# Weight requests queued behind the reads of turned softmax weights, in a two-layer attention trunk on one core

## The chip, the cores and the metric

One core of a Trainium2 chip runs the whole program. The metric is device time in microseconds (us) of one execution. The kernel before took 809.79 us (median of 3 runs, 808.65 to 813.39).

## The reference, cut to what matters

Two layers of a gated hybrid trunk on 512 rows of 1024 values, all in float32. Each layer normalises its rows, multiplies them by one wide matrix, and feeds the pieces to two branches: a sparse attention with eight heads, and a gated linear attention with four heads. The branches are multiplied up, gated, added, multiplied by an output matrix, normalised and added to the input.

```python
def _layer(x, ...):
    h = _rms(x, g_pre)
    proj = h @ w_in
    ...
    o_nsa = _nsa_attention(q_rope, q_nope, k_cmp, v_cmp, k_slc, v_slc, k_win, v_win, nsa_gate)
    o_nsa = o_nsa * jax.nn.silu(p_nz)
    ...
    o_gla = (o_gla * jax.nn.silu(p_gr...))
    m_nsa, m_gla = jnp.split(jax.nn.sigmoid(p_mg), N_BRANCHES, axis=-1)
    y = m_nsa * (o_nsa @ w_up_nsa) + m_gla * (o_gla @ w_up_gla)
    return x + _rms(y @ w_out, g_post)
```

The sparse attention of a row is three softmax branches (compressed, selected, window), each weighted by a gate. The selected and the window branch are what this change touches: their softmax weights are computed with the rows on the partitions, and have to be turned so that the keys lie on the partitions before they can multiply the values.

## The kernel before, in words

**Weights.** All weights of a layer lie packed in one tensor `wpk`, in the order of their use, as 128x1024 blocks (512 KB) or 128x512 blocks (256 KB). `load(i)` (L125) requests block i: one DMA on SyncE's queue (SP) into one of three `raw` buffers (L136), then a cast on ScalarE that keeps the high part (`A.copy`, L153) and a subtraction on VectorE that leaves the low part (L154), into two of six `hl` buffers. `split3` (L175) then makes three matmuls of each 128x128 piece: high by high (L177), high by low (L178), low by high (L179). So the first matmul of a block needs its cast, and the third needs its subtraction. `get` (L171) is called when a product starts, and requests two blocks ahead of the one that it hands out.

**Attention.** For each of four head pairs p, a step of compressed attention (`cmp_steps`, L887) is followed by four steps of `attn_steps` (L980): two halves of the rows (ip = 0, 1) by two branches (br = 0, 1). A step multiplies queries by keys (`scores`, L957), makes softmax weights (`weigh`: L970 on VectorE, the exponential L972 on ScalarE, L974 and L975 on VectorE), and turns them (`turn`, L924). Turning is a 32x32 transposition on VectorE into a tile `T` (L935), a write of that tile to DRAM (`tp`, L940) and four reads that bring it back with the keys on the partitions (`PT`, L943). The four reads are 224 KB each for the second half of the rows and 96 KB each for the first. After them the weights multiply the values (L998). In what follows "the write" is L940 and "the reads" are the four of L943.

**Order.** TensorE's order is written by hand: `go` makes one step of attention, and `fill` puts pieces of weight products between the steps, from a queue of products. A product's tanh (L593 or L736) or its copy out (L698) on ScalarE follows its last matmul. On the other engines and on SP a scheduler orders the instructions by what it thinks will be ready, unless an `issue_after` puts one behind another on its engine. The list `back` holds the reads issued so far in a layer; in `turn` a write already stands behind the latest read (L939).

**Names.** In the layer's order of blocks the ones that this text speaks of are q3, nz2, nz3 (query and gate of heads), mgg0 to mgg7 (512 KB) alternating with ug0 to ug7 (256 KB), and mgn0, un0 and so on. In the first layer q3 is `raw_1684`, nz2 `raw_1780`, nz3 `raw_1866`, ug1 `raw_2214`, mgg2 `raw_2283`, ug3 `raw_2494`, ug4 `raw_2642`, mgg5 `raw_2690`, ug6 `raw_2901`, ug7 `raw_3049`, mgn0 `raw_3097`. A product of mgg multiplies the tile `hT`, one of ug the tile `oT`.

Of the kernel before, what the change touches and what calls it, by code (L numbers as in the profile page):

```python
# [67 lines left out]
def trunk(ctx, tc, x, wpk, sp, gvec, cs, wa, out):  # L68
# [23 lines left out]
    def new(pl, shape=(128, 512), dt=F32, tag=None, bufs=None):  # L92
        cnt[0] += 1
        kw = {} if bufs is None else {"bufs": bufs}
        return sb[pl].tile(list(shape), dt, tag=tag or pl, name=f"{tag or pl}_{cnt[0]}", **kw)
# [10 lines left out]
    dma = nc.sync.dma_start  # L106
# [13 lines left out]
    POS = {k: i for i, k in enumerate(SEQ)}  # L120
    ready = {}
    issued = [0]
    first_w, behind = [], []

    def load(i):  # L125
        l, n = SEQ[i]
        off, w = OFF[n]
        src = wpk[l][:, off:off + w]
        if n.startswith("w1"):
            t = [new("a"), new("a")]  # L130
            for h in range(2):
                dma(t[h], src[:, h * 512:(h + 1) * 512])
            ready[l, n] = t
            return
        r = new("raw", (128, 1024))
        dma(r[:, :w], src)  # L136
        if i < 3:
            ready[l, n] = (new("hl", (128, 1024), F32R), new("hl", (128, 1024), F32R))
            first_w.append((r, w) + ready[l, n])
            return  # L140
        if n.startswith("wo") or n in ("gv0", "gv3", "gq0", "gk0"):
            pl = "a" if n < "wo4" and n > "wo" else "oT"
            parts = []
            for h in range(2):
                H, Lo = new(pl, dt=F32R), new(pl, dt=F32R)
                rr = r[:, h * 512:(h + 1) * 512]
                A.copy(H, rr)
                V.tensor_sub(Lo, rr, H.bitcast(F32))
                parts.append((H, Lo))
            ready[l, n] = parts  # L150
            return
        H, Lo = new("hl", (128, 1024), F32R), new("hl", (128, 1024), F32R)
        A.copy(H[:, :w], r[:, :w])  # L153
        V.tensor_tensor(Lo[:, :w], r[:, :w], H[:, :w].bitcast(F32), op=OP.subtract)  # L154
        ready[l, n] = (H, Lo)
# [9 lines left out]
    def issue(i):  # L165
        while issued[0] <= min(i, len(SEQ) - 1):
            with behind_tokens() if issued[0] < 7 else nullcontext():
                load(issued[0])
            issued[0] += 1
# [142 lines left out]
    for l in range(L):  # L312
# [21 lines left out]
        def fill(us):  # L334
            credit[0] += us
            while credit[0] > 0.3 and queue:
                credit[0] -= step(*queue[0])

        def step(name, gen):
            try:  # L340
                return next(gen)
            except StopIteration:
                queue.pop(0)
                done.add(name)
                return 0.0

        def need(name):
            while name not in done:
                step(*queue[0])
# [381 lines left out]
        def up(f, gate, wn, src, then):  # L731
            th = []

            def sig(o):
                th.append(new("th"))
                A.activation(th[0], o, AF.Tanh, scale=0.5)  # L736

            yield from fm(l, f"{gate}{f}", hT, sig)
            w = get(l, f"{wn}{f}")
            u = ps("mm")  # L740
            for k in range(4):
                sl = slice(k * 128, (k + 1) * 128)
                split3(u, (w[0][:, sl], w[1][:, sl]), src[k], k == 0, k == 3)
                if k == 3:
                    then(th[0], u)
                yield 0.64
# [172 lines left out]
            mm(acc, vbd[1], pcT, start=False, stop=False, skip_group_check=True)  # L919
            yield  # L920

        PT, TT, held, back, nsc = {}, {}, {}, [], [0]

        def turn(p, br, i, pps):  # L924

# [96 lines left out]
        def take_un(f):  # L1022
            def g(th, u):
                t_ = new("p")
                V.scalar_tensor_tensor(t_, th, 1.0, u, op0=OP.add, op1=OP.mult)  # L1025
                G.tensor_tensor(t_, t_, y2[f], op=OP.add)  # L1026
                if f < 3:
                    both = new("PT", (128, 2, 512), F32R, tag="PT1") if f < 2 else new("T", (128, 2, 512), F32R, tag="T1")
                    H, Lo = both[:, 0], both[:, 1]
                else:  # L1030
                    H, Lo = new("g", dt=F32R), new("g", dt=F32R)
                A.mul(H, t_, 0.5)
                V.scalar_tensor_tensor(Lo, t_, 0.5, H.bitcast(F32), op0=OP.mult, op1=OP.subtract)
                yT.append((H, Lo))
            return g


        for n in range(len(steps)):
# [21 lines left out]
                go(n - 2)  # L1060
            fill(f4[3])
        need("ug7")

        uns = [up(f, "mgn", "un", oTn, take_un(f)) for f in range(8)]
        for f in range(2):
# [9 lines left out]
        src = x if l == 0 else x1  # L1075
# [112 lines left out]
```

## Time and profile before

| | |
|---|---|
| median of 3 runs | 809.79 us (808.65 to 813.39) |
| the profiled execution | 808.68 us, span of its instructions 807.0 us |
| TensorE busy | 789.5 us, 98% |
| VectorE busy | 553.5 us, 69% |
| ScalarE busy | 354.4 us, 44% |
| mean granted TensorE clock | 0.997 of 2.4 GHz |

The span is the time from the first to the last instruction; the execution is 1.7 us longer. A row of a group of instructions gives the line, the engine, the operation, the output and input tiles, shapes and count, then busy time and mean ns of one, then the idle time of the engine just before them and what ended it.

### The profile page before, as it was taken

The page shows a single profiled execution, that of the slowest core. Times are in us where ns is not written, and L with a number is a line of the kernel's source. Part 1 is how long each engine was busy: PE and PEld are TensorE (multiplying, and loading weights), DVE is VectorE, ACT ScalarE, POOL GpSimd, SP SyncE. Part 2 cuts the span into 40 slices and gives each one's busy share as a digit, 9 for nine tenths or more (in the row PEclk, how much of TensorE's full clock was granted, in tenths as well). Part 3 has the DMA queues.
Part 4 walks back from the last instruction along what each step waited for, and adds up shares of the span by engine and source line. Part 5 has one row for each costly group of instructions (what it writes and reads, how often), then busy time and mean ns, then how long its engine had stood idle before and what let it go on. Part 6 is the DMA issues. An engine that isn't in the chain of part 4 may idle for free. (4 is left out here: it accounts for less than half of the span.)

```text
span 807.0 us, 12043 instructions
## 1 busy us (share of the span) xinstructions
PE 789.5 (98%) x4262; PEld 644.4 (80%) x4262; DVE 553.5 (69%) x1274; ACT 354.4 (44%) x731; POOL 97.6 (12%) x117
## 2 busy tenths in 40 slices
PE   8999999999989999999999999999999999999996
PEld 5888788887878887888898878888877788788885
DVE  6753749999998945645574366589999987366223
ACT  5671236554554524442356413556555444245211
POOL 3000024000010102211010102311000101032100
PEclk9999999999999999999999999999999999999998
DMA  6641124367676773446246121234767677545222
GB/s 233 229 147 58 53 67 130 105 191 217 183 236 204 235 227 119 153 153 223 79 129 212 52 78 54 83 114 149 223 201 215 214 212 222 171 157 158 78 105 79
DMA packets 54272, 124.04 MB, mean 154 GB/s; under 512 B 6562, under 2 KB 23490, under 8 KB 54212
## 3 DMA queue, kind: packets, MB, share of 16 engines
q1 hardware_dynamic: 54064, 123.01, 48.4%
q8 instruction: 34, 0.56, 0.3%
q10 hardware_dynamic: 148, 0.27, 0.1%
q14 instruction: 26, 0.21, 0.1%
HBM read 94.94 MB, written 25.17 MB: 149 GB/s over the span
## 5 line engine op out<-in xcount | busy, mean ns | idle before, releaser
L177 PE MATMUL ps_mm<-hT,hl 128*128 128x512 f32 x544 | 217.5, 400 | 0.0
L178 PE MATMUL ps_mm<-hT,hl 128*128 128x512 f32 x544 | 212.5, 391 | 0.0
L179 PE MATMUL ps_mm<-hT,hl 128*128 128x512 f32 x544 | 212.3, 390 | 0.0
L153 ACT CAST hl<-raw 128x1024 fp32r<-128x1024 f32 (+3 forms) x107 | 97.6, 915 | 138.3 <-PE ps_mm L178 99.9
L154 DVE TENSOR_TENSOR hl<-raw,hl 128x1024 fp32r<-128x1024 f32 (+3 forms) x107 | 117.4, 1098 | 47.6 <-ACT hl L153 42.5
L177 PEld LDWEIGHTS ps_mm<-hT,hl 128*128 128x128 f32 x544 | 102.2, 188 | 23.3 <-issue 3.1
L179 PEld LDWEIGHTS ps_mm<-hT,hl 128*128 128x128 f32 x544 | 102.2, 188 | 22.1
L178 PEld LDWEIGHTS ps_mm<-hT,hl 128*128 128x128 f32 x544 | 102.4, 188 | 19.0
L972 ACT ACTIVATE g<-g,sx 128x128 f32<-128x128 f32 (+3 forms) x128 | 71.0, 555 | 67.9 <-DVE sx L970 67.5
L935 DVE STREAM_TRANSPOSE T<-g 128x256 f32<-128x256 f32 (+3 forms) x128 | 58.6, 491 | 0.7
L975 DVE TENSOR_SCALAR g<-g,sx,gt 128x128 f32<-128x128 f32 (+3 forms) x128 | 57.0, 459 | 1.5
L178 PE MATMUL ps_mm<-oT,hl 128*128 128x512 f32 x128 | 50.3, 393 | 1.7 <-POOL oT L1006 1.7
L177 PE MATMUL ps_mm<-oT,hl 128*128 128x512 f32 x128 | 50.9, 398 | 0.0
L179 PE MATMUL ps_mm<-oT,hl 128*128 128x512 f32 x128 | 49.9, 390 | 0.0
L1006 POOL TENSOR_TENSOR oT<-p,oT 128x512 fp32r<-128x512 f32 x8 | 14.3, 1784 | 239.0 <-ACT oT L1005 239.0
L998 PE MATMUL ps_o<-PT,a 128*64 128x256 f32 (+1 forms) x384 | 38.6, 348 | 3.9 <-DMA PT<-tp 3.9
L998 PEld LDWEIGHTS ps_o<-PT,a 128*64 128x64 f32 x384 | 25.4, 137 | 18.3 <-issue 9.4
L200 POOL TENSOR_TENSOR rs<-ms,mhalf 128x1 f32<-128x1 f32 (+1 forms) x24 | 17.2, 719 | 177.0 <-DVE ms L198 175.3
L1026 POOL TENSOR_TENSOR p<-p,g 128x512 f32<-128x512 f32 x16 | 28.0, 1750 | 84.3 <-DVE p L1025 72.7
L970 DVE CUSTOM_DVE_ANT_0 g<-ps_t,cmask 128x256 f32<-128x256 f32 (+3 forms) x64 | 28.8, 477 | 2.3 <-PE ps_t L957 2.2
L970 DVE CUSTOM_DVE_ANT_0 g<-ps_s,cmask 128x128 f32<-128x128 f32 (+3 forms) x64 | 29.0, 481 | 1.7 <-PE ps_s L957 1.7
L178 PEld LDWEIGHTS ps_mm<-oT,hl 128*128 128x128 f32 x128 | 24.1, 188 | 6.5 <-POOL oT L1006 2.3
(269 smaller groups left out, 1313.3 us busy)
## 6 DMA issues: line engine op xcount, KB each, us to landing
raw<-wpk SPq DMA_DIRECT2D x96, 512.0 KB, 3.8
tp<-T SPq DMA_DIRECT2D x16, 896.0 KB, 4.1
PT<-tp SPq DMA_DIRECT2D x64, 224.0 KB, 4.9
raw<-wpk SPq DMA_DIRECT2D x32, 256.0 KB, 3.0
tp<-T SPq DMA_DIRECT2D x16, 384.0 KB, 2.5
PT<-tp SPq DMA_DIRECT2D x64, 96.0 KB, 2.4
a<-wpk SPq DMA_DIRECT2D x16, 256.0 KB, 5.7
p<-x SPq DMA_DIRECT2D x16, 256.0 KB, 2.9
```

Of the source, the lines that this page charges most:

```text
L153: A.copy(H[:, :w], r[:, :w])
L154: V.tensor_tensor(Lo[:, :w], r[:, :w], H[:, :w].bitcast(F32), op=OP.subtract)
L177: mm(o, w[0], h[0], start=first, stop=False)
L178: mm(o, w[0], h[1], start=False, stop=False)
L179: mm(o, w[1], h[0], start=False, stop=last)
L200: G.tensor_tensor(r[:, :n], ms[:, :n], mhalf[:, :n], op=OP.pow)
L935: V.transpose(t[:, :, :, g], pps[g][:, :n * 128].rearrange("p (j b q) -> p b j q", j=n, b=4))
L970: V.tensor_tensor_reduce(pp[:, :w], ob, cmask[:, 512 - w:512], 1.0, -3 * NEG, OP.add, OP.min, sx[:, 0:1])
L972: A.activation(pp[:, :w], pp[:, :w], AF.Exp, bias=sx[:, 0:1], scale=-1.0, accum_out=sx[:, 1:2])
L975: V.tensor_scalar(pp[:, :w], pp[:, :w], sx[:, 2:3], gt[:, i, h * 3 + 1 + br:h * 3 + 2 + br], op0=OP.mult, op1=OP.mult)
L998: mm(acc[g * 64:(g + 1) * 64, (i0 + 2) * 128 - w:(i0 + 2) * 128], vsw[j // 2][:, j % 2, c0:c0 + 64], m, start=False, stop=(br == 1 and j = ...
L1026: G.tensor_tensor(t_, t_, y2[f], op=OP.add)
```

## The change

A request for a 128x1024 or 128x512 weight block is put behind the latest read of turned softmax weights on SP, if there is one in this layer. The list of reads is made once instead of once per layer, and emptied when the last of the `ug` products is done, so that requests after that, and the next layer's, stand free again. Nothing else is edited; lines behind the edit in `load` have moved by one. The blocks of `w1` (L132), which go another way, are not put behind anything.

```diff
-    first_w, behind = [], []
+    first_w, behind, back = [], [], []
...
         r = new("raw", (128, 1024))
-        dma(r[:, :w], src)
+        with tc.issue_after(back[-1]) if back else nullcontext():
+            dma(r[:, :w], src)
...
-        PT, TT, held, back, nsc = {}, {}, {}, [], [0]
+        PT, TT, held, nsc = {}, {}, {}, [0]
...
         need("ug7")
+        back.clear()
```

TensorE's and GpSimd's orders stay as they are. Those of SP, ScalarE and VectorE move.

First, SP in the middle of the first layer's attention, from ug1's request to a set of reads, before:

```order
L136 DMA raw_2214<-wpk 128x512
L136 DMA raw_2283<-wpk 128x1024
L943 DMA PT_416_2020<-tp_2018 32x4x192 x4
L940 DMA tp_2085<-T_423_2045 128x768
L136 DMA raw_2342<-wpk 128x512
L943 DMA PT_433_2087<-tp_2085 32x4x192 x4
L940 DMA tp_2187<-T_440_2119 128x1792
L136 DMA raw_2396<-wpk 128x1024
L136 DMA raw_2494<-wpk 128x512
L943 DMA PT_457_2189<-tp_2187 32x4x448 x4
L940 DMA tp_2276<-T_470_2242 128x1792
L136 DMA raw_2558<-wpk 128x1024
```

and the same place now:

```order
L944 DMA PT_433_2087<-tp_2085 32x4x192 x4
L137 DMA raw_2151<-wpk 128x1024
L941 DMA tp_2187<-T_440_2119 128x1792
L944 DMA PT_457_2189<-tp_2187 32x4x448 x4
L137 DMA raw_2214<-wpk 128x512
L941 DMA tp_2276<-T_470_2242 128x1792
L944 DMA PT_479_2278<-tp_2276 32x4x448 x4
L137 DMA raw_2283<-wpk 128x1024
L137 DMA raw_2342<-wpk 128x512
L137 DMA raw_2396<-wpk 128x1024
```

The request for mgg2 (`raw_2283`) stood ahead of the reads PT_416; it now stands behind the reads PT_479, four sets of reads later. ug1 (`raw_2214`) moved past three sets.

Second, ScalarE where q3's block is cast (`hl_1686<-raw_1684`), in the first head pair of the first layer, before:

```order
L153 CAST hl_1686<-raw_1684 128x1024
L593 ACTIVATE th_1653<-ps_mm_1590 128x512
L704 CAST a_1578<-p_1575 64x512
L704 CAST a_1581<-p_1575 64x512
L972 ACTIVATE g_1664,sx_1663<-g_1664,sx_1663 128x256
L972 ACTIVATE g_1670,sx_1669<-g_1670,sx_1669 128x256
L153 CAST hl_1782<-raw_1780 128x1024
```

and now:

```order
L973 ACTIVATE g_1812,sx_1811<-g_1812,sx_1811 128x384
L973 ACTIVATE g_1818,sx_1817<-g_1818,sx_1817 128x384
L594 ACTIVATE th_1835<-ps_mm_1786 128x512
L973 ACTIVATE g_1846,sx_1845<-g_1846,sx_1845 128x512
L973 ACTIVATE g_1852,sx_1851<-g_1852,sx_1851 128x512
L154 CAST hl_1686<-raw_1684 128x1024
```

The cast of q3 has moved behind ten exponentials, the last of them (`g_1846`, `g_1852`) those of the scores that TensorE makes just ahead of q3's own product.

Third, ScalarE where ug4's block is cast (`hl_2644<-raw_2642`), in the third head pair, before:

```order
L153 CAST hl_2644<-raw_2642 128x512
L736 ACTIVATE th_2619<-ps_mm_2564 128x512
L972 ACTIVATE g_2628,sx_2627<-g_2628,sx_2627 128x384
L972 ACTIVATE g_2634,sx_2633<-g_2634,sx_2633 128x384
L153 CAST hl_2692<-raw_2690 128x1024
```

and now:

```order
L973 ACTIVATE g_2676,sx_2675<-g_2676,sx_2675 128x512
L902 ACTIVATE g_2722<-g_2722 128x256
L737 ACTIVATE th_2747<-ps_mm_2696 128x512
L154 CAST hl_2644<-raw_2642 128x512
```

The cast of ug4 now stands behind `th_2747`, the tanh of mgg4's product, and mgg4's product is the one directly ahead of ug4's on TensorE.

## Rows read from the trace of the kernel before

**Rows 1.** The page: busy time, share and instructions of each engine.
```profile
PE 789.5 (98%) x4262; PEld 644.4 (80%) x4262; DVE 553.5 (69%) x1274; ACT 354.4 (44%) x731; POOL 97.6 (12%) x117
```
**Rows 2.** Stretch, the first layer's attention: length, busy time by engine, PEclk, DMA share, GB/s.
```profile
148.00:300.00 152.00, 149.94 (x795) 121.17 (x794) 134.32 (x399) 75.10 (x184) 9.75 (x6) 1.00 0.67 204
```
**Rows 3.** Waits of TensorE: us in total, times, longest.
```profile
PE ps_o L998 <- DMA PT<-tp: 3.9, 2, 2.1
```
**Rows 4.** Waits of SP's queue, same columns.
```profile
SPq L136 <- DVE hl L154: 266.0, 71, 17.1
```
**Rows 5.** Groups by shape: cast, subtraction, tanh; busy, mean ns, idle before.
```profile
L153 ACT CAST hl<-raw 128x1024 fp32r<-128x1024 f32 x72 | 75.2, 1049 | 96.4 <-PE ps_mm L178 77.1 <-issue 12.8 <-ACT g L972 3.7
...
L153 ACT CAST hl<-raw 128x512 fp32r<-128x512 f32 x32 | 19.8, 619 | 40.9 <-PE ps_mm L178 22.8 <-issue 18.1
...
L154 DVE TENSOR_TENSOR hl<-raw,hl 128x1024 fp32r<-128x1024 f32 x72 | 92.5, 1287 | 29.8 <-ACT hl L153 28.7
...
L736 ACT ACTIVATE th<-ps_mm 128x512 f32<-128x512 f32 x32 | 18.9, 591 | 13.4 <-PE ps_mm L179 13.4
```
**Rows 6.** DMA issues: count, KB each, median us from issue to landing.
```profile
raw<-wpk SPq DMA_DIRECT2D x96, 512.0 KB, 3.8
tp<-T SPq DMA_DIRECT2D x16, 896.0 KB, 4.1
PT<-tp SPq DMA_DIRECT2D x64, 224.0 KB, 4.9
raw<-wpk SPq DMA_DIRECT2D x32, 256.0 KB, 3.0
tp<-T SPq DMA_DIRECT2D x16, 384.0 KB, 2.5
```
**Rows 7.** Timeline around mgg2's first matmuls: start us, us, instruction.
```profile
218.18 0.34 SPq L940 DMA_DIRECT2D tp<-T  x1
...
218.71 0.40 PE L177 MATMUL ps_mm<-hT,hl 128*128 128x512 f32 x1
...
219.18 0.40 PE L179 MATMUL ps_mm<-hT,hl 128*128 128x512 f32 x1
...
225.40 1.80 SPq L943 DMA_DIRECT2D PT<-tp  x4
```
**Rows 8.** Timeline: the write ahead of mgg5's and mgn0's first matmuls.
```profile
251.58 0.34 SPq L940 DMA_DIRECT2D tp<-T  x1
...
257.36 0.40 PE L177 MATMUL ps_mm<-hT,hl 128*128 128x512 f32 x1
...
287.92 0.34 SPq L940 DMA_DIRECT2D tp<-T  x1
...
292.14 0.39 PE L177 MATMUL ps_mm<-hT,hl 128*128 128x512 f32 x1
```
**Rows 9.** Timeline: q3's first matmul, and the last exponential ahead of its moved cast.
```profile
170.95 0.39 PE L177 MATMUL ps_mm<-hT,hl 128*128 128x512 f32 x1
...
175.45 0.72 ACT L972 ACTIVATE g<-g,sx 128x512 f32<-128x512 f32 x1 [0.24 <-DVE sx L970]
```
**Rows 10.** Timeline: the write ahead of ug3's first matmul.
```profile
235.55 0.34 SPq L940 DMA_DIRECT2D tp<-T  x1
...
242.30 0.40 PE L177 MATMUL ps_mm<-oT,hl 128*128 128x512 f32 x1
```
**Rows 11.** Clock: a pause in attention, the last matmul, the stretch after it.
```profile
232.29 1.74 PE L998 MATMUL ps_o<-PT,a 128*64 128x256 f32 x16 [2.06 <-DMA PT<-tp]
...
800.09 0.28 PE L1097 MATMUL ps_mm<-oT,g 128*128 128x256 f32 x1
...
802.30:807.00 4.70, 0.00 (x0) 0.00 (x0) 1.54 (x3) 0.00 (x0) 0.00 (x0) 0.50 0.31 112
```
**Rows 12.** The same filler matmul within 0 to 10.36 us, and within 10.5 to 28.
```profile
L399 PE MATMUL ps_o<-p 128*128 128x512 bf16 x5 | 2.5, 629 | 2.6 <-DVE p L393 2.6
...
L399 PE MATMUL ps_o<-p 128*128 128x512 bf16 x3 | 1.0, 379 | 0.0
```

## The prediction
> **What bounds the kernel now.** I read the table of engines first: TensorE is busy 98% of the span, no other engine over 69% [rows 1]. That is a mean, so next the stretch that the change touches: in the first layer's attention TensorE works 149.94 of 152 us, at full clock [rows 2]. Then the waits of TensorE: in both layers' attention it waits for one thing only, the reads of turned weights, twice, 3.9 us in all [rows 3]. So there is almost nothing to win here, and everything to lose: any block of weights that comes late stops the engine that sets the time.
>
> Then why blocks are never late. SP spends 266 us in front of weight requests waiting for a `raw` buffer to be split [rows 4], and the casts wait for TensorE to give back `hl` buffers, 77.1 us for the large blocks [rows 5]. So a block lies in `raw` before its cast can start, and is split while TensorE still has earlier blocks to work on. The early request is the cover for landing (3.8 us), cast (1.05) and subtraction (1.29) [rows 5, 6].
>
> **What the change does to that.** It moves requests on SP only; no bytes or matmuls are added, and TensorE's order stays. But a request now stands behind reads that stand behind a write that needs transposed tiles, which need scores that TensorE makes only shortly before it wants the block. The cover becomes a chain: write lands (4.1 us for the 896 KB tile, 2.5 for the 384 KB one), four reads are issued (1.8 us) [rows 7], the block lands, and is cast [rows 5, 6].
>
> How long a block takes to land right behind the four reads the trace does not show. From below it is its own median, 3.8 us; from above the median of those reads, 4.9 us [rows 6], plus what little it adds. I take 4.9, since four reads of 224 KB are on the same queue ahead of it; with 3.8 the sum below would be 7 us smaller. The Trainium skill (DMA: Bandwidth & Descriptors, section on queues, rings and completion order) says that each DMA engine consumes the descriptors of a queue in their order, which speaks for the upper value; no row here shows a request in that place.
>
> So the chain from a large write to the end of the cast is 4.1 + 1.8 + 4.9 + 1.05 = 11.9 us. TensorE wants mgg2 0.53 us after that write is issued (218.18 to 218.71) [rows 7], mgg5 5.78 us after its write, and mgn0 4.22 us after its own [rows 8]. They are late by 11.3, 6.1 and 7.6 us. A short wait of about 1.5 us (below) lies between the scores and the block in each case and takes that much off: 9.8, 4.6, 6.1. Then the third matmul wants the low part 0.47 us after the first [rows 7], but the subtraction ends 1.29 us after the cast [rows 5]: 0.8 us more each. That makes 10.6, 5.4 and 6.9, together 22.9 us.
>
> **q3** is late for another reason. The scheduler, which now takes the block to land late, has put its cast behind ten exponentials. The last of them ends at 175.45 + 0.72 = 176.2, so the cast ends at 177.2, and TensorE wants the block at 170.95 [rows 9]: 6.3 us late, 7.1 with the low part. Those exponentials need scores that TensorE makes just ahead, so this cannot be hidden.
>
> **Short waits.** The casts of ug1, ug4 and ug7 now stand behind the tanh of the product directly ahead (the third pair of order rows): TensorE is idle for tanh 0.59 and cast 0.62, and the low part, half of 1.29 less 0.47, adds 0.2: 1.4 each, 4.2 for three. nz2 and nz3 stand in the same way behind the copy or tanh of the product ahead, with a large block: 0.59 + 1.05 + 0.8 = 2.4 each, 4.9 for two [rows 5]. ug3 follows a small write: 2.5 + 1.8 + 3.0 + 0.62 = 7.9 against 6.75 us (235.55 to 242.30) [rows 10], 1.2 late, 1.4 with the low part; ug6 stands alike, together 2.8. ug5, mgg3, mgg4, mgg6 and mgg7 stand behind the same reads but are wanted a product or two later; I cost them at nothing, because the waits ahead of them have already given them the time.
>
> **Sum.** One layer: 22.9 + 7.1 + 4.2 + 4.9 + 2.8 = 41.9 us; two layers 84. The two waits for reads [rows 3] should go, since reads no longer stand behind requests that wait for buffers: minus 4. That is 80.
>
> **Clock.** The four long waits per layer are idle times of 5 to 10 us. A pause of 2.06 us in attention left the clock full; after the last matmul, issued at 800.09, the clock stands at 0.50, that is at 1.2 of 2.4 GHz, in the stretch from 802.3 [rows 11]. So I expect the long waits to drop it. At the lower level a filler matmul took 629 ns instead of 379 [rows 12]. What a drop costs is open: nothing from below; from above half of the 7.8 us from the first matmul (2.6) to 10.36 [rows 12], that is 3.9. After a long wait TensorE runs densely, unlike at the start, so I take 1.5 each, 12 for eight.
>
> The profiled execution took 808.7 us, 1.1 below the median of the three runs. 808.7 + 80 + 12 = **901 us**, slower by 11%. A difference of 0.5% (4 us) is about what a measurement of this kernel can tell from none.
>
> **Rivals.**
> - *It does what its name suggests.* The reads come out from behind the requests, the 3.9 us of waits go, and the blocks still come in time: 805 us. This decides if the chain of 11.9 us fits into the time by which a block is ready early. For it: casts wait for TensorE, not for loads [rows 5]. Against: mgg2 is wanted 0.53 us after a write that must land before its request is even issued [rows 7]. Chance 0.01.
> - *It does nothing*, if the edge is without effect: 808.7. The order rows show the requests moved. 0.01.
> - *Only the long waits stay.* SP no longer stands blocked ahead of writes, tiles are transposed a little sooner as VectorE has fewer subtractions among them, and the short casts find gaps: two layers of 22.9 + 7.1, less 3.3 for three blocks that land in 3.8, and no clock loss: 808.7 + 2 x 26.7 - 4 = 858. Chance 0.12.
> - *The clock costs its upper bound.* All eight long waits drop it and each costs 3.9: 31 instead of 12, 920 us; with further waits behind matmuls that last longer, up to 932. For it: the idle times are more than twice the pause that did no harm [rows 11]. The Trainium skill (TensorE: Matmul & The Clock Gate, part 1) says that an idle engine falls to the lower level and only sustained work lifts it again; by that rule every long wait would pay. Chance 0.22.
>
> **How the numbers follow.** My own sum has 0.64. Its range: from below no clock loss (minus 12), landing at 3.8 (minus 7) and tiles done about 1.5 us sooner in each of eight long waits (minus 12): 870. From above the clock rival, 932. 870 to 932 takes in these two cases, 0.86, without the other three. Faster by over 0.5%: 0.01; within: 0.01; slower: 0.98.
>
> **What would show it.** In the profile of the changed kernel TensorE should wait some 80 to 90 us, nearly all of it at L178 to L180 (one line further down) for ScalarE's cast and VectorE's subtraction of `hl`, in eleven places per layer; the four longest, in front of q3, mgg2, mgg5 and mgn0, of 5 to 10 us each. SP should no longer wait for subtractions ahead of weight requests in attention but for writes ahead of reads. The waits for PT should be gone. The granted clock should fall below 0.99, with dips behind the long waits. Time outside attention, from wo on, should be unchanged. It would be wrong if TensorE's waits in attention stay under 40 us, if ScalarE's casts still wait for TensorE there, or if the new waits stand at L999 for the reads.

## The result, and the profile after

The changed kernel takes 911.3 us (median of 4 runs, 909.44 to 913.38); the kernel before, on the same chip, 810.49 us (808.65 to 813.39). The ratio is 1.1235 (95% interval 1.1206 to 1.1265): slower by 12%, where 901 us, within 870 to 932, was forecast. The profiled execution took 909.6 us; its span is 907.9 us, 100.9 longer than before.

First the page's table of engines and two rows of its costliest groups, which answer to [rows 1] and [rows 5]:

```profile
PE 819.4 (90%) x4262; PEld 652.8 (72%) x4262; DVE 563.4 (62%) x1274; ACT 356.2 (39%) x731; POOL 93.5 (10%) x117
...
L178 PE MATMUL ps_mm<-hT,hl 128*128 128x512 f32 x544 | 224.6, 413 | 54.8 <-ACT hl L154 54.8
...
L178 PE MATMUL ps_mm<-oT,hl 128*128 128x512 f32 x128 | 52.2, 408 | 16.1 <-ACT hl L154 16.1
```

The same 4262 matmuls keep TensorE busy 29.9 us longer (789.5 before), and it stands idle 71 us longer (88.5 against 17.5). Nearly all of that idle time stands in front of the first matmul of a product, for a cast. The waits of TensorE and of SP's queue (us in total, times, longest), to be held against [rows 3, 4]:

```profile
PE ps_mm L178 <- ACT hl L154: 71.0, 22, 7.4
PE ps_mm L180 <- DVE hl L155: 4.0, 7, 1.1
```
```profile
SPq L137 <- DVE hl L155: 192.9, 53, 17.1
SPq L941 <- DVE T L936: 138.3, 26, 11.8
SPq L944 <- DMA tp<-T: 75.8, 28, 4.1
```

The wait for the reads is gone, 75.0 us of waits for casts and subtractions have come. SP's queue stands less in front of requests (266.0 before) and more in front of writes and reads. All 22 waits for casts lie in attention, eleven in each layer. The first layer's, in the timeline of TensorE (start, duration, instruction, idle time before it and what ended it):

```profile
176.72 0.80 PE L178 MATMUL ps_mm<-hT,hl 128*128 128x512 f32 x1 [5.96 <-ACT hl L154]
178.29 0.80 PE L180 MATMUL ps_mm<-hT,hl 128*128 128x512 f32 x1 [0.36 <-DVE hl L155]
...
189.97 0.50 PE L178 MATMUL ps_mm<-hT,hl 128*128 128x512 f32 x1 [1.67 <-ACT hl L154]
191.46 0.51 PE L180 MATMUL ps_mm<-hT,hl 128*128 128x512 f32 x1 [0.76 <-DVE hl L155]
...
199.93 0.50 PE L178 MATMUL ps_mm<-hT,hl 128*128 128x512 f32 x1 [2.18 <-ACT hl L154]
201.75 0.50 PE L180 MATMUL ps_mm<-hT,hl 128*128 128x512 f32 x1 [1.09 <-DVE hl L155]
...
232.71 0.50 PE L178 MATMUL ps_mm<-oT,hl 128*128 128x512 f32 x1 [1.25 <-ACT hl L154]
243.87 0.80 PE L178 MATMUL ps_mm<-hT,hl 128*128 128x512 f32 x1 [7.38 <-ACT hl L154]
...
269.48 0.50 PE L178 MATMUL ps_mm<-oT,hl 128*128 128x512 f32 x1 [2.21 <-ACT hl L154]
284.73 0.50 PE L178 MATMUL ps_mm<-oT,hl 128*128 128x512 f32 x1 [1.19 <-ACT hl L154]
293.65 0.80 PE L178 MATMUL ps_mm<-hT,hl 128*128 128x512 f32 x1 [5.14 <-ACT hl L154]
...
319.92 0.50 PE L178 MATMUL ps_mm<-oT,hl 128*128 128x512 f32 x1 [2.21 <-ACT hl L154]
332.52 0.50 PE L178 MATMUL ps_mm<-oT,hl 128*128 128x512 f32 x1 [1.19 <-ACT hl L154]
341.49 0.80 PE L178 MATMUL ps_mm<-hT,hl 128*128 128x512 f32 x1 [5.68 <-ACT hl L154]
```

From top to bottom these are q3, nz2, nz3, ug1, mgg2, ug3, ug4, mgg5, ug6, ug7 and mgn0: 38.3 us in this layer, 36.7 in the second. The chain behind the longest of them, mgg2, in the timelines of SP, ScalarE, VectorE and TensorE:

```profile
219.44 0.87 PE L958 MATMUL ps_s<-a,a 128*128 128x384 f32 x4
...
230.96 0.34 SPq L941 DMA_DIRECT2D tp<-T  x1
234.85 2.08 SPq L944 DMA_DIRECT2D PT<-tp  x4
237.03 1.32 SPq L137 DMA_DIRECT2D raw<-wpk  x3
...
242.78 1.56 ACT L154 CAST hl<-raw 128x1024 fp32r<-128x1024 f32 x2 [5.20 <-DMA raw<-wpk]
...
243.85 1.83 DVE L155 TENSOR_TENSOR hl<-raw,hl 128x1024 fp32r<-128x1024 f32 x2 [4.91 <-ACT hl L154]
```

Scores, write, reads, request, landing, cast: TensorE stops at 236.49, a little before the request for what it needs is even issued (237.03). Not every wait is of this kind. In ScalarE's timeline of the first layer the cast itself waits for its load at nz3, mgg2, mgg5 and mgn0, 21.5 of the 38.3 us. At q3, nz2 and the five ug blocks, 16.8 us, it starts without waiting for a load, right behind exponentials, a tanh or a copy on ScalarE, as at q3:

```profile
174.93 0.71 ACT L973 ACTIVATE g<-g,sx 128x512 f32<-128x512 f32 x1
...
175.63 1.03 ACT L154 CAST hl<-raw 128x1024 fp32r<-128x1024 f32 x1
```

The clock, by stretches (length, TensorE's busy time, granted clock, DMA share, GB/s): two of the ten stretches at half clock in attention, two waits of the same length, and the work after the second of them. The last row is the middle of the program (with VectorE, ScalarE and GpSimd too).

```profile
240.62:247.42 6.80, 3.51 (x9) 0.50 0.47 175
267.27:269.48 2.21, 0.01 (x1) 1.00 0.98 412
271.35:274.75 3.40, 3.40 (x10) 0.50 0.76 218
...
317.71:319.92 2.21, 0.00 (x0) 1.00 0.98 412
319.92:326.00 6.08, 6.00 (x33) 1.00 0.75 167
...
363.00:608.00 245.00, 243.71 (x1330) 203.17 (x1328) 151.34 (x276) 104.64 (x194) 37.34 (x43) 1.00 0.36 116
```

Before, TensorE's clock in attention was full throughout [rows 2]. Now it is at 0.50, that is at 1.2 of 2.4 GHz, in ten stretches of 3.4 to 10.2 us, 61.2 us together, all of them around or behind a wait; TensorE is busy 43.75 us of them. Between the two layers' attention nothing has changed: TensorE works 243.71 of these 245 us, and as much of the same stretch before (310.2 to 555.2).

### The profile page after: what moved, and what is told of

It is laid out like the page before. It is cut to its first block, busy times and chain, and to the rows that moved or that the text cites. A ratio compares the mean times of both kernels' runs of the same rounds, so it can differ in the third digit from the quotient of the medians.

```text
span 907.9 us, 11990 instructions
## 1 busy us (share of the span) xinstructions
PE 819.4 (90%) x4262; PEld 652.8 (72%) x4262; DVE 563.4 (62%) x1274; ACT 356.2 (39%) x731; POOL 93.5 (10%) x117
## 5 line engine op out<-in xcount | busy, mean ns | idle before, releaser
L178 PE MATMUL ps_mm<-hT,hl 128*128 128x512 f32 x544 | 224.6, 413 | 54.8 <-ACT hl L154 54.8
L180 PE MATMUL ps_mm<-hT,hl 128*128 128x512 f32 x544 | 218.5, 402 | 4.2 <-DVE hl L155 4.0
L179 PE MATMUL ps_mm<-hT,hl 128*128 128x512 f32 x544 | 217.5, 400 | 0.0
L178 PEld LDWEIGHTS ps_mm<-hT,hl 128*128 128x128 f32 x544 | 105.4, 194 | 83.0 <-ACT hl L154 59.9
L180 PEld LDWEIGHTS ps_mm<-hT,hl 128*128 128x128 f32 x544 | 105.0, 193 | 34.3 <-DVE hl L155 11.8
L179 PEld LDWEIGHTS ps_mm<-hT,hl 128*128 128x128 f32 x544 | 105.6, 194 | 19.3
L178 PE MATMUL ps_mm<-oT,hl 128*128 128x512 f32 x128 | 52.2, 408 | 16.1 <-ACT hl L154 16.1
L936 DVE STREAM_TRANSPOSE T<-g 128x256 f32<-128x256 f32 (+3 forms) x128 | 62.3, 500 | 1.1
L180 PE MATMUL ps_mm<-oT,hl 128*128 128x512 f32 x128 | 51.5, 402 | 0.3
L179 PE MATMUL ps_mm<-oT,hl 128*128 128x512 f32 x128 | 50.8, 397 | 0.6 <-POOL oT L1007 0.6
L1007 POOL TENSOR_TENSOR oT<-p,oT 128x512 fp32r<-128x512 f32 x8 | 10.3, 1286 | 328.8 <-ACT oT L1006 328.8
L999 PE MATMUL ps_o<-PT,a 128*64 128x256 f32 (+1 forms) x384 | 40.6, 363 | 0.0
```

Source lines behind the costliest of these rows:

```text
L178: mm(o, w[0], h[0], start=first, stop=False)
L179: mm(o, w[0], h[1], start=False, stop=False)
L180: mm(o, w[1], h[0], start=False, stop=last)
L936: V.transpose(t[:, :, :, g], pps[g][:, :n * 128].rearrange("p (j b q) -> p b j q", j=n, b=4))
L999: mm(acc[g * 64:(g + 1) * 64, (i0 + 2) * 128 - w:(i0 + 2) * 128], vsw[j // 2][:, j % 2, c0:c0 + 64], m, start=False, stop=(br == 1 and j = ...
```

## The experiments

Theory A, the prediction's own: a block is late because its request is; the request stands behind reads, these behind a write, this behind TensorE's own scores; and the clock falls in the waits. Below the first two rows each kernel is the changed one with one edit; each ratio is to runs of the kernel before on the same chip, whose medians lie between 809.7 and 811.0. "Waits" is what TensorE waits for casts and subtractions of `hl` at the two lines shown above, with the longest; "busy" is TensorE's busy time less the 789.5 us of before. Both are of the profiled execution.

| kernel | us | ratio to before (95%) | waits, longest | busy |
|---|---|---|---|---|
| before | 810 | | 0 | 0 |
| the change | 911.3 | 1.1235 (1.1206 to 1.1265) | 75.0, 7.4 | +29.9 |
| one set earlier | 880.9 | 1.0875 (1.0849 to 1.0902) | 46.6, 4.4 | +28.4 |
| two sets earlier | 831.8 | 1.0264 (1.0247 to 1.0281) | 16.9, 2.4 | +9.2 |
| three sets earlier | 803.8 | 0.992 (0.9905 to 0.9936) | 0 | -1.6 |
| four sets earlier | 810.1 | 1.0005 (0.999 to 1.0019) | 0 | +0.5 |
| mgg2 alone | 831.0 | 1.0258 (1.0238 to 1.0278) | 22.2, 11.4 | +5.5 |
| ug1, ug4, ug7 alone | 840.6 | 1.0379 (1.0351 to 1.0406) | 25.2, 3.4 | +17.0 |
| first layer alone | 860.8 | 1.0626 (1.0582 to 1.0671) | 37.8, 7.5 | +16.5 |
| one block further ahead | 874.9 | 1.0781 (1.0755 to 1.0807) | 41.5, 3.0 | +30.1 |
| casts first | 910.0 | 1.1239 (1.1207 to 1.127) | 74.1, 7.7 | +30.2 |
| fillers in the waits | 896.8 | 1.1079 (1.105 to 1.1107) | 25.7, 1.5 | +9.9 besides the fillers |

**Which reads.** A request may go ahead of the latest set of four reads, of two sets, of three:

```diff
-        with tc.issue_after(back[-1]) if back else nullcontext():
+        with tc.issue_after(back[-5]) if len(back) > 4 else nullcontext():
```

(`back[-9]` and `back[-13]` with 8 and 12 for two and three sets.) One set:

> A request may go ahead of the latest set of four reads and stands behind the set before it; nothing else is edited. Theory A (the time comes from where a request stands against the writes and reads: write, reads, landing, cast, TensorE): the four longest waits lose the time that the reads take ahead of the request, which in the changed kernel is some 4 to 6 us of each, so mgg2, mgg5 and mgn0 fall from 7.1, 4.9 and 5.5 us to about 1 to 4 us, q3 likewise; several of the 1 to 2.6 us waits stay or shift to other blocks because requests still wait for a write. The extra 101 us shrink to 40 to 70, so 850 to 880 us. Rival B (ScalarE's order decides: casts stand behind exps and tanhs that the scheduler puts ahead of them, whenever the block lands): nothing much is gained, 890 to 911. Rival C (the slow clock is a state that any wait of over 1 us brings, whatever its length): waits shrink but TensorE's busy time stays near 819 us, 870 to 890.

Two sets:

> A request stands behind the reads two sets before the latest; nothing else is edited. Theory A: one set more is one write-and-read round (some 10 us) earlier, more than the longest wait of the changed kernel (7.4 us), so the four long waits are gone and at most four or five waits of 1 to 3 us are left in a layer; the extra time falls to 5 to 25 us over the kernel before, 815 to 835, and TensorE's busy time comes back to within 8 us of 789.5. Rival B (ScalarE's order): over 870. Rival C (any wait drops the clock): 835 to 850 with busy time over 800.

Three sets:

> A request stands behind the reads three sets before the latest; nothing else is edited. Theory A: requests are issued about where the kernel before issues them, so no TensorE wait for a cast or subtraction is left in attention; what may be left of the change's own effect is that no request runs ahead of reads that TensorE waits for, so the 3.9 us of waits for turned softmax weights go: 804 to 809 us, ratio 0.994 to 1.000 to the kernel before. Rival D (those waits came from the write before the reads, not from requests ahead of them): no difference, 807 to 812. Rival B: over 850.

The time falls by 30, 49 and 28 us with each set, and with three it is below the kernel before. That a block's lateness is its request's place is borne out; rival B, which has ScalarE's order alone decide, would have kept each of them near the changed kernel. That order was not held fixed, though: the scheduler moves the casts with the requests (q3's cast starts at 175.63 us in the changed kernel, at 167.68 with one set, at 154.99 with two), so what it adds at the blocks that have landed is not told apart here. (The expectation's 7.1, 4.9 and 5.5 us are 7.4, 5.1 and 5.7 in the timeline above.) One set came out 0.9 us above A's range, and for the reason that rival C gave: the waits fell by 28 us, but TensorE's busy time hardly moved.

With three sets TensorE waits neither for casts nor for turned weights. SP's queue ahead of the reads that TensorE waits for in the first layer before (its wait ends at 232.29, [rows 11]; write and reads in [rows 7]), with the scores of that write and the subtraction that frees a buffer, in the timelines of the kernel before

```profile
203.64 0.87 PE L957 MATMUL ps_s<-a,a 128*128 128x384 f32 x4
...
219.09 6.20 SPq L136 DMA_DIRECT2D raw<-wpk  x2
...
223.74 1.19 DVE L154 TENSOR_TENSOR hl<-raw,hl 128x1024 fp32r<-128x1024 f32 x1
```

and with three sets, with the page's table of engines:

```profile
PE 787.9 (98%) x4262; PEld 643.0 (80%) x4262; DVE 552.6 (69%) x1274; ACT 353.4 (44%) x731; POOL 97.5 (12%) x117
...
217.57 0.34 SPq L941 DMA_DIRECT2D tp<-T  x1
218.01 1.35 SPq L137 DMA_DIRECT2D raw<-wpk  x2
222.16 2.72 SPq L944 DMA_DIRECT2D PT<-tp  x4
```

Before, the second of two requests waited for a free buffer, and the two held the queue for 6.20 us (the subtraction was done at 224.93), so that the reads came 7.22 us after the write; the write needs about 4.1 [rows 6]. With three sets the two requests take 1.35 us, and the reads come 4.59 us after the write. To see whether it is that, or any order set by hand, the same edit with four sets:

> A request stands behind the reads four sets before the latest. With three sets the kernel was 7 us faster than the kernel before, with no wait left for turned softmax weights. Theory A (that gain comes from SyncE's queue: in the kernel before a request that waits for a free buffer stands in front of reads that are ready): with four sets SyncE's rows are nearly those of the kernel before, a waiting request stands in front of reads again, the waits for turned weights come back (3 to 4 us) and the time is 807 to 812, ratio 0.996 to 1.002. Rival J (any order by tokens is faster, because the scheduler places other work better with it): 801 to 806.

```profile
PE ps_o L999 <- DMA PT<-tp: 4.6, 2, 2.6
```
```profile
218.55 0.34 SPq L941 DMA_DIRECT2D tp<-T  x1
219.45 6.19 SPq L137 DMA_DIRECT2D raw<-wpk  x2
225.76 1.80 SPq L944 DMA_DIRECT2D PT<-tp  x4
```

The time in the queue (6.19 us) is back, the wait for turned weights (4.6 us) is back, and so is the time of the kernel before. So the idea in the change's name is right, and worth 0.8%, at one distance: behind the reads three sets back, where the request no longer blocks reads that are ready and still comes in time.

**One long wait alone.** Only mgg2's request stands behind the latest reads:

```diff
-        with tc.issue_after(back[-1]) if back else nullcontext():
+        with tc.issue_after(back[-1]) if back and n == "mgg2" else nullcontext():
```

> Only mgg2's request, one block in each layer, stands behind the latest reads; SyncE's queue is served in order, so requests behind it are late too, but by what this one costs. Theory A: one wait of 7 us at mgg2 in each layer, some 1.5 to 4 us of slow clock behind it, and up to 3 us at the blocks whose requests follow it: 14 us of waits and 3 to 10 us in all of other cost, 825 to 835 us. Rival E (the long waits build on each other: mgg2 is late only because the requests ahead of it are): under 815. Rival F (one wait stops the whole chain of requests for the rest of the layer): over 850.

```profile
PE ps_mm L178 <- ACT hl L154: 22.2, 2, 11.4
```
```profile
204.13 0.87 PE L958 MATMUL ps_s<-a,a 128*128 128x384 f32 x4
...
217.90 0.34 SPq L941 DMA_DIRECT2D tp<-T  x1
...
230.77 0.79 PE L178 MATMUL ps_mm<-hT,hl 128*128 128x512 f32 x1 [11.41 <-ACT hl L154]
```

The total is as A said, but not its parts: nothing else waits, and the one wait is 4.0 us longer than in the change. Two things account for most of that. In the change the tiles are turned sooner, 11.5 us from the start of the scores to the write (219.44 to 230.96) against 13.8 here (204.13 to 217.90); and TensorE is held up 1.25 us at ug1 in between. So the waits of one chain share their time: they can't be measured singly and added.

**Three short waits alone.** The same edit with `n in ("ug1", "ug4", "ug7")`:

> Only ug1, ug4 and ug7 stand behind the latest reads, the three whose waits are 1.2 us each in the changed kernel (7 us in both layers). Theory A in the form that the single block mgg2 has shown (alone it waited 11.4 us and in company 7.4, because there TensorE came later): the three wait longer alone than in company, 3 to 6 us each, or the blocks whose requests queue behind theirs do, so 18 to 36 us with the clock, 829 to 847. Rival I (waits add up block by block, each with the length that it has in the changed kernel): 7 to 10 us, 818 to 821.

840.6 us: the edit at three blocks that show 1.2 us each in the change costs 31 us, three to four times what rival I makes of them. Not all of it lies at the three: in the first layer they wait 3.4, 1.4 and 2.5 us, and the `mgg` and `mgn` blocks behind them, on whose requests there is no edge, another 5.4. (The profiled execution was one of 846.1 us, so the waits and busy time in the table are a little above those of the median.) Again the length of a wait in the changed kernel isn't what its block costs.

**Which layer.** The edge only where `l == 0`:

> Only the first layer's requests stand behind the latest reads. Theory A (the cost is made anew in each layer, 11 waits each): half of the 101 us, 855 to 865, with the second layer as in the kernel before and eleven waits in the first. Rival L (lateness is carried on from layer to layer): the second layer's blocks are late too, over 870.

860.8 us, half of the loss; the first layer has its eleven waits for casts, the second none.

**Request a block earlier.**

```diff
-    def get(l, n, ahead=2):
+    def get(l, n, ahead=3):
```

> The changed kernel, with each block's request written one block earlier (three blocks ahead of its use where it was two), still behind the latest reads at that place. Theory A (a block is late because its request is): a block's request then stands behind the reads of an earlier place in most cases, one block of TensorE's work earlier (some 3 to 6 us), which is most of a long wait; 840 to 880 us, with mgg2, mgg5 and mgn0 under 4 us each. Rival K (a request could not go earlier anyway, since it waits for a free buffer that the block before gives up): 895 or more.

874.9 us, as A said; no wait is over 3.0 us. But TensorE's busy time is 30.1 us above before, as much as with waits of 7.4.

**ScalarE's order.** The tanh or copy that ends a product goes behind the cast of the next block:

```diff
-        A.copy(H[:, :w], r[:, :w])
+        cast[i] = A.copy(H[:, :w], r[:, :w]).ins
...
-                then(o)
+                nxt = cast.get(POS[l, n] + 1) if back else None
+                with tc.issue_after(nxt) if nxt else nullcontext():
+                    then(o)
```

> The changed kernel, with ScalarE's tanh or copy at the end of a block put behind the cast of the next block's weights, where it stood ahead of it; SyncE's and TensorE's rows are the same. Theory A (a block is late because its bytes are late): only the short waits in which tanh or copy (0.58 us) stands ahead of a block that has landed shrink, ug1, ug4, ug7 and nz2, by up to 0.6 us each, 5 us in both layers, and some of it is lost again to a later gate or drain: 903 to 913. Rival B (ScalarE's order, not the landing, makes most of the 70 us of waits): over 25 us gained, under 886.

```profile
PE ps_mm L178 <- ACT hl L154: 70.2, 14, 7.7
```

The waits for casts are 14 instead of 22, and with those for subtractions they sum to the same within 0.9 us: what a short wait no longer takes, a later one does. So where tanh and copy stand on ScalarE places the loss and doesn't make it. The exponentials were not moved; behind them q3, ug3 and ug6 still wait 5.4, 2.4 and 2.2 us in the first layer. No run moves them while the requests stay late.

**The clock.** Matmuls whose results are overwritten, ahead of the first real one of the eight blocks that wait longest:

```diff
+FILLERS = {"q3": 24, "nz2": 6, "nz3": 9, "mgg2": 30, "mgg5": 20, "mgn0": 23, "ug3": 8, "ug6": 8}
...
+        for _ in range(FILLERS.get(n, 0)):
+            mm(o, ident_b, cmask, start=True, stop=True)
```

> The changed kernel, with 512-column bf16 matmuls whose results are overwritten put ahead of the first real matmul of the eight blocks in a layer that wait over 1.6 us (24 at q3, 6 at nz2, 9 at nz3, 30 at mgg2, 20 at mgg5, 23 at mgn0, 8 each at ug3 and ug6: 256 in all, some 0.22 us each, 56 us); the waits stay as long as they are, but TensorE works through them. Theory A (the 30 us by which TensorE's busy time grew are matmuls at the half clock, on the path that sets the end): the clock goes back to 0.99 or more and the time falls by 15 to 28 us, to 883 to 896; what is left over the kernel before, 70 to 85 us, is the waits alone. Rival G (the slowed matmuls lie where TensorE would have waited anyway, since the slower it is the later it comes to the next wait): the clock comes back but the waits grow by as much, 903 to 915. Rival H (the clock falls with what the change does to the transfers, and not with TensorE's pauses): the clock stays at 0.965, and the fillers cost time, 911 to 930.

In the timeline around mgg2 (its matmuls stand one line further down in this kernel):

```profile
236.05 6.65 PE L188 MATMUL ps_mm<-cmask,ident_b 128*128 128x512 bf16 x29
243.00 0.50 PE L179 MATMUL ps_mm<-hT,hl 128*128 128x512 f32 x1 [0.30 <-ACT hl L155]
...
244.26 0.50 PE L181 MATMUL ps_mm<-hT,hl 128*128 128x512 f32 x1 [0.53 <-DVE hl L156]
```

The granted clock is 0.996 (0.965 without), and 14.5 us come back (911.3 to 896.8), 0.8 less than A's range begins with. So of the 101 us, the late blocks make 87 at full clock and the clock 14.5. That is half of the 29.9 us by which the busy time grew. The stretches at half clock hold 43.75 us of work, so no more than half of these, 21.9 us, could come back. Of the 21.9 a part only fills a wait: at full clock TensorE is ready for a block's low part sooner than VectorE, the 0.53 us above, which the changed kernel doesn't show at mgg2; such waits sum to 8.4 us here, where they were 4.0. The other 8 us of busy time are not the clock's: ahead of the end the clock is at 0.50 for 3.4 us only here, and TensorE, busy for 855.6 us, 56.25 of them with fillers, still works 9.9 us longer than before. An estimate of where it goes: a wait ends a dense row of matmuls, which start 0.23 us apart, with one that is seen in full, 0.39 us (236.10, ahead of mgg2), and begins the next with one whose successor comes after 0.34 (232.71, at ug1). That is 0.27 us for each wait, 7.8 for the 29 of the changed kernel and 9.2 for the 34 that are left here; no run tests it. Rivals G and H fall.

## Why the prediction was right

The direction and its cause were right: eleven places in each layer, the four longest at q3, mgg2, mgg5 and mgn0, TensorE waiting for casts because requests stand behind a chain that it feeds itself, or, at q3, because the cast stands behind exponentials of scores that it makes just ahead. By the prediction's steps:

- **The chain** was put at 11.9 us and took 12.9 at mgg2, from the write (230.96) to the end of the first cast (243.8): 3.9 until the reads are issued, 2.2 to issue them, 5.7 until the block has landed, 1.05 to cast. A request right behind four reads lands in 5.7 us, above the 4.9 taken, and far above the 3.8 that the alternative gave. The Trainium skill (DMA: Bandwidth & Descriptors, section on queues, rings and completion order) has each DMA engine take a queue's descriptors in their order; the trace agrees, since the reads ahead of mgg2's block, the last of them issued at 236.50, land 3.4 us after issue (median) and the block after them, at 242.7. What of the 5.7 us is this order and what is the load on the engines no run separates.
- **The waits**, predicted and measured in the first layer: mgg2 10.6 and 7.4; mgg5 5.4 and 5.1; mgn0 6.9 and 5.7; q3 7.1 and 6.3; nz2 and nz3 4.9 and 5.7; ug1, ug4 and ug7 4.2 and 3.6; ug3 and ug6 2.8 and 4.4. Together 41.9 and 38.3. At mgg2 the tiles were turned 3.0 us sooner than before (14.5 us from scores to write then, 203.64 to 218.18, and 11.5 now), which the prediction had only in its lower bound; the cause, fewer subtractions in VectorE's way, was argued and not tested. The low part's 0.8 us at mgg2, mgg5 and mgn0 is missing because the half clock hides it. At ug3 and ug6 the step was wrong, as the rows below show: the block, requested at 259.86, had landed 3.1 us later, and its cast stood behind exponentials until 268.82. At nz3, too: what its cast waited for last was the load, not a tanh.
- **The clock** was put at 12 us, 1.5 for each of eight waits. The fillers give 14.5. All eight long waits did drop it, and two shorter ones as well: 1.45 us for each of ten. The 1.5 was chosen between 0 and 3.9, so that it fits is luck. And the 3.9 rests on the start of the program, taken to be at the lower level; the profile's clock column has 1.00 there (0 to 10.36 us), so that only the 629 ns against 379 speak for it. The Trainium skill (TensorE: Matmul & The Clock Gate, part 1) says that an idle engine falls to the lower level; the trace agrees for each long wait, but the rival built on it, 31 us, is out: all the work at half clock, 43.75 us, could give back 21.9 at most. The 12 us more in the range's upper end, 920 to 932, come from no row.
- **The sum**: waits were put at 84 us, 80 without those for reads. In the changed kernel they are 75.0 and 71, a little under the 80 to 90 named as a sign; at full clock, with the fillers counted as waiting, they are 82 (56.25 and 25.7) and 78. So this term fits, in part by luck: mgg2's wait came out 3.2 us shorter, those at ug3 and ug6 1.6 longer. What the sum left out is busy time that grows at full clock, 9.9 us by the fillers; with the 2.5 us by which the clock was put too low, and less 2 by which the waits were put too high, it is the distance from 901 to 911 us.
- **The rivals** with blocks in time, or with no effect, are excluded; that only the long waits stay (858) too: the short ones did not find gaps.
- **The minus 4** for reads that no longer stand behind blocked requests was right, and the one useful part of the change: with three sets it is what is left, 5.0 us by the spans of the profiled executions (807.0 to 802.0): TensorE stands idle 3.4 us less, since these waits are gone and others grew a little, and is busy 1.6 us less. The clock, full in attention in both, has no part in it.

ScalarE's casts, said to wait no more for TensorE in attention, wait there for loads alone, as the waits of ScalarE from 148 to 347 us show; from 148 to 300 us before, they waited 10.7 us for TensorE and for no load:

```profile
ACT hl L154 <- DMA raw<-wpk: 17.5, 8, 7.9
```

ug3, in the changed kernel's DMA issues from 259 to 262 us, and in its timeline of SP and ScalarE:

```profile
raw<-wpk SPq DMA_DIRECT2D x1, 256.0 KB, 3.1
```
```profile
259.86 0.85 SPq L137 DMA_DIRECT2D raw<-wpk  x2
...
268.22 0.60 ACT L973 ACTIVATE g<-g,sx 128x384 f32<-128x384 f32 x1
...
268.82 1.55 ACT L154 CAST hl<-raw 128x512 fp32r<-128x512 f32 x2
```

## What to carry to other kernels

Before a prefetch is put behind other transfers, follow what these wait for: if that is the very engine which the prefetch feeds, the prefetch's cover turns into a chain, and a block comes a whole chain (here 12.9 us from the write on) after work that the engine itself has only just done. The opposite fault is a prefetch that waits for a buffer at the head of a queue and holds back transfers that are ready; the cure for both is a fixed distance, here three sets of reads, found by trying one, two, three and four. The lengths of waits in such a chain don't add up: taken alone, three blocks with 1.2 us of wait each cost 31 us in two layers, with what queues behind them, and a wait of 7.4 us became 11.4.

## What was not expected of the hardware

The work at half clock did not follow the length of the waits. With waits of at most 3.0 us (a block further ahead) TensorE was busy at half clock for 49.7 us, in eleven stretches; with waits of up to 7.4 us (the change) for 43.75, in ten; with two waits of 11.4 and 10.8 us (mgg2 alone) for 11.3, in two. So 30 waits of at most 3 us put more work at half clock than two long ones; what that costs in time was measured for the change alone. Nor does one length decide: behind the 2.21 us wait at 267.27 the clock fell to 0.50 after TensorE had already worked again for 1.9 us; behind the one of equal length at 317.71 it stayed at 1.00. What tells these two apart no run here shows.
